# Inverse blocks of a head fetched in four transfers and spread by ScalarE and GpSimd; rotary halves exchanged by ScalarE copies

## The chip, the cores and the metric

The kernel runs on one NeuronCore of one Trainium2 chip. A core has five engines that each work through their own list of instructions in order and meet only at semaphores: TensorE (PE in the profile, with its weight loads as PEld) multiplies, VectorE (DVE), ScalarE (ACT) and GpSimd (POOL) work elementwise, and SyncE (SP) issues the transfers (DMA) between the chip's memory, HBM, and the on-chip memory, SBUF. Results of TensorE land in PSUM, a small accumulator memory. The metric is the device time of one execution in microseconds (us), taken as the median of several runs.

## The reference

One layer of a hybrid encoder on a sequence of 1024 tokens, width 1024, float32: a mixer (windowed attention beside a gated delta rule in both directions), cross-attention into 256 memory tokens, and a SwiGLU feed-forward part. What the change touches lies in the mixer. The queries and keys of the attention are rotated:

```python
def _rope(x, positions):
    ...
    x1, x2 = xf[..., :half], xf[..., half:]
    return jnp.concatenate([x1 * cos - x2 * sin, x2 * cos + x1 * sin], axis=-1)
```

and each chunk of the delta rule solves a triangular system, which the kernel does by inverting the matrix:

```python
    lower = jnp.where(strict, jnp.einsum('bhnid,bhnjd->bhnij', kb, k) * decay, 0.0)
    tmat = lower + jnp.eye(c, dtype=jnp.float32)
    ...
    sol = lax.linalg.triangular_solve(tmat, rhs, left_side=True, lower=True, unit_diagonal=True)
```

## The kernel before

Large products run as three TensorE products of a high and a low part of each operand (`split`, L99: ScalarE rounds the high part, VectorE or GpSimd subtracts the low part). The program goes through five parts: the normalized input is transposed; the delta projections (`delta_proj`) run with the preparation of each head; then comes the part that the change touches; then the scan over eight steps of 128 tokens with attention windows and the memory's keys and values in between; then the output projection, cross-attention and feed-forward part, which fill the time after some 570 us.

The part in question follows the table `ORDER_2` (L37): `L0 L1 G0 G1 A4 V A0 A1 L2 L3 W W W A2 A3 G2 G3 W`. `A` is an attention projection (`attn_proj`, 128 of the query or key columns, with the rotation), `V` the value projection, `G` a gate projection, `W` two attention windows, and `L` is `levels(h)`, which builds the inverse of the triangular matrices of head `h` (of four) out of inverses of 32 x 32 blocks. The table sets only the order in which code is written; a scheduler then orders the instructions of each engine by its own model of their times, and each engine keeps that order on the chip. All transfers of this part are issued by SP, one after the other. An instruction on any engine that waits holds up all that stand behind it on that engine.

`base_inverse(g)` (L503) inverts the 32 x 32 blocks of two heads on VectorE, in a chain of small steps (L534, L536) that ends with two scaled copies V (L538) and A (L539). Four transfers (L543) store them to `d_inv`, for g = 0 before this part and for g = 1 (heads 2 and 3) inside it. GpSimd takes part in that chain with one instruction before its steps (L528) and one after them (L537).

`levels(h)` then needs the blocks of one head in several places of 128 x 128 tiles: `D5` and `D6` (from set 0) and `Z0`, `Z1` and `m5` (from set 1). D5, D6, Z0 and Z1 exist once and are used by one head after the other; their zeros between the blocks stay from one head to the next. Each of the four row groups q of 32 partitions is fetched by a transfer of its own: 5 per q, 20 per head, 80 in all. After that come two rounds of small products (`pair`: L585, a copy `bs` by ScalarE at L587, and L591) with copies between the blocks by ScalarE and VectorE, and the finished Z0 and Z1 are stored to `d_pz` (L610), from where the scan reads them.

`attn_proj` has two halves of 512 tokens, each in a PSUM bank `pg`. The rotation multiplies with the sine (`sn`, L729), then the halves of 32 rows trade places by four transfers within SBUF (L734), while the product with the cosine (`rop`, L730) waits to be added to what comes back (L735). The sum is split into a high and a low part, and both are stored to `d_q` or `d_k` (L739), from where the windows load them as `qs`, `khi` and `klo` (L679, L625). `sn` lies in a buffer with the tag `rot`, of which two exist and which the value projection uses too, for `vT` (L745, L746).

Of the kernel before, what the change touches and what calls it, by code (L numbers as in the profile page):

```python
# [10 lines left out]
F32 = mybir.dt.float32  # L11
# [3 lines left out]
ALU = mybir.AluOpType  # L15
# [4 lines left out]
P = 128  # L20
# [3 lines left out]
NT = S // P  # L24
HALF = 512
# [7 lines left out]

ORDER_1 = "D0 P0 D1 P1 D2 B0 P2 D3 P3 B1".split()
ORDER_2 = "L0 L1 G0 G1 A4 V A0 A1 L2 L3 W W W A2 A3 G2 G3 W".split()  # L37
ORDER_3 = ("M " + "s01 W K " * 5 + "s01 K " * 3 + "s01 V V").split()
# [4 lines left out]
_ROPE_AT = len(_NAMES) * P  # L43
# [3 lines left out]
def host_constants():  # L47
    i = np.arange(P)
    blk = i // 32
    a, b = i[:, None], i[None, :]  # L50
    ba, bb = blk[:, None], blk[None, :]
    tri = {
        "ident": a == b,
        "mU": a < b,
        "mL": a > b,
        "mUi": a <= b,
        "mLi": a >= b,
        "m5": (ba // 2 == bb // 2) & (ba != bb),
        "m6": ba // 2 != bb // 2,
        "ones": a + b >= 0,  # L60
    }
    out = np.zeros((P, _NCONST), np.float32)
    for n, m in tri.items():
        out[:, _AT[n]:_AT[n] + P] = m

    out[:, _AT["band0"]:_AT["band0"] + P] = np.where(b >= a, 0.0, NEG)
    out[:, _AT["band2"]:_AT["band2"] + P] = np.where(b <= a, 0.0, NEG)
    half = np.arange(32, dtype=np.float32)
    inv = np.power(np.float32(10000.0), -half / np.float32(32)).astype(np.float32)
    out[:, _ROPE_AT] = inv[i % 32]  # L70
    out[:, _ROPE_AT + 1] = np.where(i % 64 < 32, 1.0, -1.0)
    return out


# [1 line left out]
def tile_hybrid_block(  # L76
# [4 lines left out]
    g_ffn_pre, w_gate_up, w_down, g_ffn_post, consts, out, dump=None, stop=None,  # L81
):
    nc = tc.nc
    x, mem, out = x[0], mem[0], out[0]
# [64 lines left out]
    trp = p1.enter_context(pool("trp", 2, side="right"))  # L149
# [396 lines left out]
    def levels(h):  # L546

        g, hh = h // 2, h % 2

        def fetch(dst, q, i, d):  # L550
            nc.sync.dma_start(dst, d_inv[g][i][d, hh, :, q].rearrange("c r s -> r c s"))

        m5 = tl_.tile([P, NT, 32], F32, tag="m5", name="m5", bufs=1)
        D5a, D6a, *Za = wide_sets[0]
        for q in range(4):
            r = slice(32 * q, 32 * q + 32)
            fetch(m5[r], q, 1, 1 - q % 2)
            fetch(D5a[r, :, r], q, 0, q % 2)
            fetch(D6a[r, :, r], q, 0, q // 2)
            for d in range(2):  # L560
                fetch(Za[d][r, :, r], q, 1, d)

        def part(b):
            c4 = slice(4 * b, 4 * b + 4)

            def wide(name):
                return tl_.tile([P, 4, P], F32, tag=name, name=name, bufs=2)

            L5, L6 = wide("L5"), wide("L6")
            D5, D6, Z = D5a[:, c4], D6a[:, c4], [z[:, c4] for z in Za]  # L570
            Ul = wide("Ul")
            nc.sync.dma_start(Ul, d_u[g][hh, c4].rearrange("c p n -> p c n"))
            yield
            p_ = small().rearrange("p (c n) -> p c n", c=4)
            for j in range(4):
                nc.tensor.transpose(p_[:, j, :], Ul[:, j, :], ident)
            nc.vector.tensor_tensor(L5, p_, bc(cm["m5"], 1, (P, 4, P)), ALU.mult)
            nc.vector.tensor_tensor(L6, p_, bc(cm["m6"], 1, (P, 4, P)), ALU.mult)

            def pair(lt, mv, dd, w):  # L580

                yield
                p_ = small()[:, 0:4 * w].rearrange("p (c n) -> p c n", c=4)
                for c in range(4):
                    nc.tensor.matmul(p_[:, c, :], lt[:, c, :], mv[:, c, :], start=True, stop=True)  # L585
                bs = tl_.tile([P, 4, 64], F32, tag="bs", name="bs", bufs=2)[:, :, 0:w]
                nc.scalar.copy(bs, p_)  # L587
                yield
                p_ = small()[:, 0:4 * w].rearrange("p (c n) -> p c n", c=4)
                for c in range(4):  # L590
                    nc.tensor.matmul(p_[:, c, :], dd[:, c, :], bs[:, c, :], start=True, stop=True)  # L591
                return p_

            p_ = yield from pair(L5, m5[:, c4, :], D5, 32)
            z5 = tl_.tile([P, 4, 32], F32, tag="z5", name="z5", bufs=2)
            nc.scalar.mul(z5, p_, -1.0)
            nc.vector.transpose(D6[32:64, :, 0:32], z5[0:32])
            nc.vector.transpose(D6[64:96, :, 96:128], z5[96:128])
            nc.vector.tensor_copy(Z[1][32:64, :, 0:32], z5[32:64])
            nc.vector.tensor_copy(Z[0][64:96, :, 96:128], z5[64:96])  # L600
            mov6 = tl_.tile([P, 4, 64], F32, tag="mov6", name="mov6", bufs=2)
            nc.scalar.copy(mov6[0:64], Z[1][0:64, :, 0:64])
            nc.vector.tensor_copy(mov6[64:128], Z[0][64:128, :, 64:128])
            nc.scalar.copy(Z[0][0:32, :, 32:64], z5[0:32])
            nc.scalar.copy(Z[1][96:128, :, 64:96], z5[96:128])
            p_ = yield from pair(L6, mov6, D6, 64)
            nc.scalar.mul(Z[0][0:64, :, 64:128], p_[0:64], -1.0)
            nc.vector.tensor_scalar(Z[1][64:128, :, 0:64], p_[64:128], -1.0, None, ALU.mult)
            for d in range(2):
                nc.sync.dma_start(d_pz[g][d][c4, :, hh, 1].rearrange("c p n -> p c n"), Z[d])  # L610

        together([part(b) for b in range(2)])
# [108 lines left out]
    def attn_proj(ct):  # L721
        pp = proj(w_in[:, ct * P:(ct + 1) * P])
        dst = [t[ct * P:(ct + 1) * P, :] if ct < 4 else t for t in (d_q if ct < 4 else d_k)]
        for hf in range(2):
            sl = slice(hf * HALF, (hf + 1) * HALF)
            rop = trp.tile([P, HALF], F32, tag="rop", name="rop")
            sn = trp.tile([P, HALF], F32, tag="rot", name="sn")
            rot = trp.tile([P, HALF], F32, tag="rot2", name="rot2")
            nc.vector.tensor_tensor(sn, pp[hf], sinT[:, sl], ALU.mult)  # L729
            nc.vector.tensor_tensor(rop, pp[hf], cosT[:, sl], ALU.mult)  # L730

            for q in range(4):
                o = 32 * (q ^ 1)
                nc.sync.dma_start(rot[32 * q:32 * q + 32], sn[o:o + 32])  # L734
            nc.vector.tensor_tensor(rop, rop, rot, ALU.add)  # L735
            hl = [trp.tile([P, HALF], F32R, tag=t, name=t) for t in ("qhi", "qlo")]
            split(*hl, rop)
            for t, o in zip(hl, dst):
                nc.sync.dma_start(o[:, sl], f32(t))  # L739
# [623 lines left out]
    def fetch(dst, r, ch, k, n):  # L1363
        return nc.sync.dma_start(dst[:, k:k + n], wv[:, k:k + n, r, ch * 512:(ch + 1) * 512])
# [160 lines left out]
```

## Time and profile before

| what | us |
|---|---|
| median of 3 runs (lowest, highest) | 1551.69 (1547.02, 1553.25) |
| the profiled execution, its own time | 1555.78 |
| its span from first to last instruction | 1554.1 |
| TensorE busy in the span | 1497.3 |
| VectorE busy | 1055.9 |
| ScalarE busy | 719.6 |
| GpSimd busy | 308.3 |

An engine's busy time counts its computing instructions, not waits or the issue of transfers. The page of a profile lists the busy time of each engine, a strip of 40 equal slices, the DMA queues, the chain of waits (what released what, followed back from the last instruction), the costliest groups of instructions and the issues of transfers. Other views list the waits, single instructions in order of time, or the work in chosen stretches of the span, with the clock that TensorE was granted there (1.00 is full speed). "SPq" is SP issuing a transfer. A row such as `L735 DVE TENSOR_TENSOR rop<-rop,rot ... x10: 679/688/693` gives line, engine, operation, what is written from what, how often, and the shortest, median and longest duration in ns.

### The profile page before, as it was taken

The numbers are of one execution on the slowest core, as the hardware profiler recorded it, in microseconds if no ns is written. First come the engines' busy times: TensorE is split into PE (matmuls) and PEld (weight loads), VectorE is DVE, ScalarE is ACT, GpSimd is POOL, SyncE is SP. The second block draws the span as 40 slices with busy tenths as digits, with TensorE's granted clock in tenths as the row PEclk, the third lists the DMA queues.
The fourth block names the chain that finished last, engine by engine and source line by source line (L and its number), as shares of the span: only waits on it lengthen the run. The fifth ranks groups of instructions, "written<-read, shape, count | busy, mean of one in ns | idle before, by whom it ended". The sixth has DMA issues, their size and how long they took to land.

```text
span 1554.1 us, 20931 instructions
## 1 busy us (share of the span) xinstructions
PE 1497.3 (96%) x7451; PEld 1258.1 (81%) x7451; DVE 1055.9 (68%) x1750; ACT 719.6 (46%) x1380; POOL 308.3 (20%) x305
## 2 busy tenths in 40 slices
PE   6999999898899999999999999999999999999998
PEld 5888888787899877888888777888888888888786
DVE  6777898766898766443447367776867554687665
ACT  6666552246556755454335574332323332454532
POOL 2000110000003201163102221433533333000021
PEclk9999999997999999999999999999999999999999
DMA  6244456867987584354213264344434334863354
GB/s 211 69 136 128 125 157 160 217 179 245 319 278 247 164 283 165 119 190 148 82 55 123 85 200 141 111 135 129 134 122 132 102 102 141 288 193 102 108 175 165
DMA packets 267366, 247.16 MB, mean 159 GB/s; under 512 B 39016, under 2 KB 204797, under 8 KB 267261
## 3 DMA queue, kind: packets, MB, share of 16 engines
q1 hardware_dynamic: 267261, 245.82, 50.7%
q8 instruction: 59, 0.97, 0.3%
q14 instruction: 46, 0.38, 0.1%
HBM read 173.65 MB, written 69.50 MB: 156 GB/s over the span
## 4 chain that ended last, share of the span: by engine, by line
PE 80%; DVE 6%; DMA 6%; ACT 3%; issue 2%; SPq 2%; POOL 0%; DVEq 0%; POOLq 0%; ACTq 0%
PE pg L261 13%; PE pmg L1016 10%; PE pD L1196 8%; PE pE L1196 8%; PE pA L1196 6%; PE pcq L261 6%; PE pdX L1386 6%; PE pdA L1386 4%; PE pB L1196 4%; PE psc L785 2%; PE pdX L1479 2%; PE pdD L1386 2%; DMA wraw<-in_w_ckv_dram 2%; PE pcs L1102 1%; PE pco L1128 1%
## 5 line engine op out<-in xcount | busy, mean ns | idle before, releaser
L102 ACT CAST whi<-wraw 128x1024 fp32r<-128x1024 f32 x108 | 113.5, 1051 | 173.3 <-PE pg L261 36.0
L103 DVE TENSOR_TENSOR wlo<-wraw,whi 128x1024 fp32r<-128x1024 f32 x78 | 95.5, 1225 | 77.7 <-ACT whi L102 75.0
L261 PE MATMUL pg<-hhi,whi 128*128 128x512 f32 x352 | 140.8, 401 | 0.2 <-DVE rop L730 0.2
L261 PE MATMUL pg<-hhi,wlo 128*128 128x512 f32 x352 | 140.2, 399 | 0.0
L261 PE MATMUL pg<-hlo,whi 128*128 128x512 f32 x352 | 139.9, 398 | 0.0
L1016 PE MATMUL pmg<-whi,b 128*128 128x512 f32 x384 | 118.4, 394 | 0.4 <-ACT b L102 0.4
L1196 PE MATMUL pA<-s,whi 128*128 128x512 f32 x352 | 109.5, 392 | 1.4 <-ACT m L1213 1.4
L103 POOL TENSOR_TENSOR wlo<-wraw,whi 128x1024 fp32r<-128x1024 f32 x30 | 73.8, 2460 | 143.3 <-ACT whi L102 143.2
L1016 PEld LDWEIGHTS pmg<-whi,b 128*128 128x128 f32 x384 | 71.3, 188 | 15.2 <-ACT b L102 1.3
L261 PEld LDWEIGHTS pg<-hhi,whi 128*128 128x128 f32 x352 | 67.3, 192 | 14.0 <-DVE rop L730 0.7
L261 PEld LDWEIGHTS pg<-hlo,whi 128*128 128x128 f32 x352 | 67.2, 191 | 13.2
L261 PEld LDWEIGHTS pg<-hhi,wlo 128*128 128x128 f32 x352 | 67.2, 191 | 13.1
L1196 PEld LDWEIGHTS pA<-s,whi 128*128 128x128 f32 x352 | 65.3, 188 | 15.2 <-ACT m L1213 2.0
L1386 PE MATMUL pdX<-dhl,whi 128*128 128x512 f32 x264 | 76.1, 390 | 1.5 <-DVE zv L1441 0.8
L1016 PE MATMUL pmg<-wlo,b 128*128 128x512 f32 x192 | 71.5, 392 | 0.0
L1196 PE MATMUL pA<-s,wlo 128*128 128x512 f32 x176 | 68.7, 392 | 1.1 <-DVE wlo L103 1.1
L102 ACT CAST whi<-araw 128x1024 fp32r<-128x1024 f32 (+1 forms) x36 | 35.4, 984 | 69.9 <-PE pdX L1386 27.6
L1273 POOL TENSOR_TENSOR act<-act,up 128x512 f32<-128x512 f32 x33 | 50.1, 1519 | 89.1 <-DVE up L1272 53.1
L103 DVE TENSOR_TENSOR wlo<-araw,whi 128x1024 fp32r<-128x1024 f32 (+1 forms) x36 | 40.8, 1133 | 38.4 <-ACT whi L102 38.3
L286 DVE SCALAR_TENSOR_TENSOR acc<-cp,cols,acc 128x1024 f32<-128x1024 f32 x48 | 61.5, 1282 | 1.5 <-ACT acc L284 0.8
L1386 PEld LDWEIGHTS pdX<-dhl,whi 128*128 128x128 f32 x264 | 49.3, 188 | 12.8 <-issue 1.1
L1246 DVE TENSOR_TENSOR sr<-sr,wraw 128x512 f32<-128x512 f32 x22 | 37.8, 1716 | 29.8 <-POOL sr L1245 29.8
(409 smaller groups left out, 3976.7 us busy)
## 6 DMA issues: line engine op xcount, KB each, us to landing
wraw<-in_w_gate_up_dram SPq DMA_DIRECT2D x52, 512.0 KB, 4.0
kv<-d_kv SPq DMA_DIRECT2D x32, 512.0 KB, 6.6
wraw<-in_w_in_dram SPq DMA_DIRECT2D x22, 512.0 KB, 5.5
b<-in_w_down_dram SPq DMA_DIRECT2D x20, 512.0 KB, 6.8
araw<-d_as SPq DMA_DIRECT2D x20, 512.0 KB, 3.8
pz<-d_pz SPq DMA_DIRECT2D x32, 256.0 KB, 6.8
wraw<-in_w_ckv_dram SPq DMA_DIRECT2D x16, 512.0 KB, 6.4
wraw<-in_w_out_dram SPq DMA_DIRECT2D x16, 512.0 KB, 4.3
```

The source lines that it names most:

```text
L102: nc.scalar.copy(hi, src)
L103: (eng or nc.vector).tensor_tensor(lo, src, f32(hi), ALU.subtract)
L261: nc.tensor.matmul(p_, w[:, k, :], ah[a][:, k, :], start=(k == 0 and i == 0), stop=(k == nk - 1 and i == 2))
L286: nc.vector.scalar_tensor_tensor(acc, cp[:, t:t + S], taps[t], acc, ALU.mult, ALU.add)
L785: nc.tensor.matmul(out[:, d, h, :], lt[:, d, h, :], rt[:, d, h, :], start=True, stop=True)
L1016: nc.tensor.matmul(pp[t], act[a][:, k, tt], w_[:, kk, :], start=(k == 0 and i == 0), stop=(k == KT - 1 and i == 2))
L1102: nc.tensor.matmul(pp[:, t2_, :], q[a][:, ct, tt], kr_[b_][:, ct, :], start=(j == 0 and i == 0), stop=(j == 1 and i == 2))
L1196: nc.tensor.matmul(out_, w[a][:, k, :], xx[b_][:, k, :], start=(start and k == 0 and i == 0), stop=(k == HK - 1 and i == 2), skip_group_ch ...
L1246: nc.vector.tensor_tensor(s[1], s[0], a_[:, 0:HK], ALU.subtract)
L1273: nc.gpsimd.tensor_tensor(o_, o_, up, ALU.mult)
L1386: nc.tensor.matmul(banks[t], a[:, k - k0, tt], w, start=(first and k == 0 and i == 0), stop=(k == NB - 1 and i == 2), skip_group_check=not ...
L1479: nc.tensor.matmul(X[t], a[:, k], w[:, k0 + k], start=False, stop=(k0 + k == NB - 1 and i == 2), skip_group_check=True)
```

## The change

The blocks of a head now come in four transfers instead of 20: each of the four sets (two of set 0, two of set 1) is fetched whole, 128 partitions x 8 chunks x 32, into a tile `c` of which four exist (`LC = 4`). From there 8 GpSimd copies put them into D5 and D6, and 12 ScalarE copies into m5, Z0 and Z1, each copy 32 partitions x 256 elements. For four heads that is 16 transfers in place of 80, 32 GpSimd copies and 48 ScalarE copies.

The rotation now begins with four ScalarE copies of 32 partitions x 512 out of PSUM, which write each group of 32 rows to the partitions of its partner group. VectorE then multiplies the copy with the sine in place, and adds as before. For five projections of two halves that is 40 ScalarE copies in place of 40 transfers; VectorE keeps three multiplications or additions per half. The sign column of the constants is turned around, since the sine is now taken at the place where the row arrives. The tile of tag `rot2` is gone.

```diff
+LC = 4
...
-    out[:, _ROPE_AT + 1] = np.where(i % 64 < 32, 1.0, -1.0)
+    out[:, _ROPE_AT + 1] = np.where(i % 64 < 32, -1.0, 1.0)
...
-        def fetch(dst, q, i, d):
-            nc.sync.dma_start(dst, d_inv[g][i][d, hh, :, q].rearrange("c r s -> r c s"))
+        def fetch(i, d):
+            t = tl_.tile([P, NT, 32], F32, tag="c", name="c", bufs=LC)
+            nc.sync.dma_start(t, d_inv[g][i][d, hh].rearrange("c b r s -> (b r) c s"))
+            return t
 
         m5 = tl_.tile([P, NT, 32], F32, tag="m5", name="m5", bufs=1)
         D5a, D6a, *Za = wide_sets[0]
+        cw = [fetch(0, d) for d in range(2)]
         for q in range(4):
             r = slice(32 * q, 32 * q + 32)
-            fetch(m5[r], q, 1, 1 - q % 2)
-            fetch(D5a[r, :, r], q, 0, q % 2)
-            fetch(D6a[r, :, r], q, 0, q // 2)
-            for d in range(2):
-                fetch(Za[d][r, :, r], q, 1, d)
+            nc.gpsimd.tensor_copy(D5a[r, :, r], cw[q % 2][r])
+            nc.gpsimd.tensor_copy(D6a[r, :, r], cw[q // 2][r])
+        cz = [fetch(1, d) for d in range(2)]
+        for q in range(4):
+            r = slice(32 * q, 32 * q + 32)
+            nc.scalar.copy(m5[r], cz[1 - q % 2][r])
+        for d in range(2):
+            for q in range(4):
+                r = slice(32 * q, 32 * q + 32)
+                nc.scalar.copy(Za[d][r, :, r], cz[d][r])
...
-            sn = trp.tile([P, HALF], F32, tag="rot", name="sn")
-            rot = trp.tile([P, HALF], F32, tag="rot2", name="rot2")
-            nc.vector.tensor_tensor(sn, pp[hf], sinT[:, sl], ALU.mult)
-            nc.vector.tensor_tensor(rop, pp[hf], cosT[:, sl], ALU.mult)
-
+            rot = trp.tile([P, HALF], F32, tag="rot", name="rot")
             for q in range(4):
                 o = 32 * (q ^ 1)
-                nc.sync.dma_start(rot[32 * q:32 * q + 32], sn[o:o + 32])
+                nc.scalar.copy(rot[32 * q:32 * q + 32], pp[hf][o:o + 32])
+            nc.vector.tensor_tensor(rop, pp[hf], cosT[:, sl], ALU.mult)
+            nc.vector.tensor_tensor(rot, rot, sinT[:, sl], ALU.mult)
             nc.vector.tensor_tensor(rop, rop, rot, ALU.add)
```

Since the scheduler orders everything anew, the change also moves instructions that it doesn't name. In the rows below the lines of the changed kernel count 1 more than before up to the change and 7 to 9 more behind it; a name's number tells buffers apart.

First, ScalarE where the blocks of head 0 and the rotation of the first projection stand. Before:

```order
L102 CAST whi<-wraw 128x1024
L758 ACT_TABLE_LOAD
L758 ACTIVATE gt<-pg 128x512
L102 CAST whi<-wraw 128x1024 x2
L587 COPY bs<-ps 128x4x32
L746 COPY vT<-pg 128x512
L587 COPY bs<-ps 128x4x32
```

And now:

```order
L739 COPY rot<-pg 32x512 x4
L103 CAST qhi<-rop 128x512
L103 CAST whi<-wraw 128x1024
L739 COPY rot<-pg 32x512 x4
L566 COPY m_2128<-c 32x256 x2
L570 COPY Z_2122<-c 32x8x32 x4
L753 COPY vT<-pg 128x512
L566 COPY m_2128<-c 32x256 x2
L570 COPY Z_2123<-c 32x8x32 x4
```

The copies of the rotation (`rot`) and of the blocks (`m`, `Z`) stand ahead of `vT`, where ScalarE had two roundings of weights.

Second, SP between the store of the inverse blocks for heads 2 and 3 and the loads of the first window. Before:

```order
L543 DMA d_inv_113<-A 64x1024
L543 DMA d_inv_114<-A 64x1024
L739 DMA d_q_98<-qhi 128x512
L551 DMA m_2832<-d_inv_114 32x8x32
L551 DMA D_2120<-d_inv_113 32x8x32
L551 DMA m_2832<-d_inv_114 32x8x32
L551 DMA D_2120<-d_inv_113 32x8x32
L739 DMA d_q_99<-qlo 128x512
L551 DMA D_2120<-d_inv_113 32x8x32
L551 DMA m_2832<-d_inv_114 32x8x32 x2
L551 DMA D_2120<-d_inv_113 32x8x32
L679 DMA khi<-d_k_100 64x1024 x2
```

And now:

```order
L544 DMA d_inv_113<-A 64x1024
L544 DMA d_inv_114<-A 64x1024
L553 DMA c<-d_inv_113 128x8x32 x2
L553 DMA c<-d_inv_114 128x8x32 x2
L688 DMA khi<-d_k_100 64x1024 x2
L688 DMA klo<-d_k_101 64x1024 x2
L634 DMA qs<-d_q_98 64x4x128
```

Eight fetches of blocks and two stores of queries between the inverse blocks and the window's keys have become four fetches; the window's loads still stand behind the store of the inverse blocks.

Third, ScalarE late in the part, where the blocks of head 3 are due, behind head 2's last copies. Before (the blocks themselves came by transfers):

```order
L667 COPY ao<-pow 64x512
L758 ACTIVATE gt<-pg 128x512
L642 ACT_TABLE_LOAD
L642 ACTIVATE sc,ssum<-sc,nm 128x384 x4
L646 ACTIVATE es<-es 128x4
L587 COPY bs<-ps 128x4x32 x2
L102 CAST ph<-ptw 128x512 x2
L758 ACT_TABLE_LOAD
L758 ACTIVATE gt<-pg 128x512
```

And now:

```order
L616 ACTIVATE Z_2122<-ps 64x4x64 x2
L676 COPY ao<-pow 64x512
L765 ACT_TABLE_LOAD
L765 ACTIVATE gt<-pg 128x512
L570 COPY Z_2122<-c 32x8x32 x4
L570 COPY Z_2123<-c 32x8x32 x4
L103 CAST ph<-ptw 128x512
L655 ACT_TABLE_LOAD
L655 ACTIVATE es<-es 128x4
L651 ACTIVATE sc,ssum<-sc,nm 128x384 x4
L765 ACT_TABLE_LOAD
L765 ACTIVATE gt<-pg 128x512
```

Eight copies into Z0 and Z1 now stand on ScalarE among the windows' exponentials, and the function tables are loaded more often: 10 times over the part where there were 6.

## The prediction

> **What bounds the kernel now.** I read the page first: busy times and the chain of waits.
>
> ```profile
> PE 1497.3 (96%) x7451; PEld 1258.1 (81%) x7451; DVE 1055.9 (68%) x1750; ACT 719.6 (46%) x1380; POOL 308.3 (20%) x305
> PE 80%; DVE 6%; DMA 6%; ACT 3%; issue 2%; SPq 2%; POOL 0%; DVEq 0%; POOLq 0%; ACTq 0%
> ```
>
> TensorE is the bound over the whole kernel, so an edit elsewhere pays only where TensorE stands still or runs at a lowered clock. The change lies between 228 and 384 us. The view by stretches shows what is to be had there; the columns are TensorE, weight loads, VectorE, ScalarE, GpSimd (busy us), then the granted clock, the DMA share and GB/s.
>
> ```profile
> 228.00:250.00 22.00, 22.00 (x103) 18.16 (x101) 18.25 (x33) 2.11 (x2) 2.26 (x1) 1.00 0.68 155
> 250.00:270.00 20.00, 17.97 (x94) 15.57 (x94) 17.08 (x40) 6.98 (x17) 0.00 (x0) 0.83 0.70 193
> 270.00:290.00 20.00, 20.00 (x112) 17.18 (x112) 15.97 (x39) 3.73 (x9) 0.16 (x1) 1.00 0.71 194
> 290.00:310.00 20.00, 16.82 (x93) 13.97 (x91) 13.56 (x25) 7.84 (x18) 0.00 (x0) 1.00 0.88 228
> 310.00:330.00 20.00, 18.25 (x92) 15.94 (x92) 10.13 (x27) 4.67 (x15) 0.20 (x1) 0.83 0.69 160
> 330.00:350.00 20.00, 19.77 (x112) 16.94 (x112) 16.28 (x42) 11.62 (x29) 0.59 (x1) 1.00 0.68 203
> 350.00:370.00 20.00, 19.27 (x117) 17.39 (x116) 11.47 (x35) 12.41 (x30) 0.20 (x1) 0.89 0.66 183
> 370.00:384.00 14.00, 10.80 (x43) 8.44 (x43) 8.29 (x21) 8.66 (x20) 2.15 (x5) 0.54 0.85 278
> 228.00:384.00 156.00, 144.88 (x755) 123.59 (x754) 111.04 (x256) 58.03 (x137) 5.56 (x10) 0.90 0.73 196
> ```
>
> TensorE is idle for 156 - 144.88 = 11.1 us, and the clock takes more: 0.17 x 20 in each of two stretches, 0.11 x 20 and 0.46 x 14, together 15.4 us. So at most 26.5 us can be won here. The lowered clock follows the idle places (250:270, 290:330, the end): a stop costs itself and then a few us at half speed.
>
> The issuing engine, SP, is what these stops have in common. Its rows for the fetches and the rotation (shortest/median/longest ns per issue):
>
> ```profile
> L551 SPq DMA_DIRECT2D D<-d_inv x32: 390/452/874, 239.4 to 352.3; - x32
> L551 SPq DMA_DIRECT2D Z<-d_inv x32: 302/449/1042, 240.4 to 359.9; - x32
> L551 SPq DMA_DIRECT2D m<-d_inv x16: 320/467/1333, 238.6 to 325.6; - x16
> L734 SPq DMA_DIRECT2D rot<-sn x40: 507/588/1240, 251.1 to 340.6; - x40
> ```
>
> By the medians that is 14.5 + 14.4 + 7.5 + 23.5 = 59.8 us of issuing in some 125 us. The waits from 228 to 385 us name what is late for it (us in total, times, longest), and the chain of waits names two longer places:
>
> ```profile
> DVE rop L735 <- DMA rot<-sn: 7.4, 5, 2.8
> ACT vT L746 <- DMA rot<-sn: 4.3, 1, 4.3
> PE psw L633 <- DMA qs<-d_q: 3.9, 1, 3.9
> 306.21 5.30 DMA qs<-d_q
> 311.75 1.19 PE psw L633 x4
> ...
> 355.25 4.63 DMA d_gate<-gt
> 359.89 2.87 DMA Z<-d_inv
> ```
>
> **The change part by part.** The sum is made against the profiled execution, 1555.78 us with a span of 1554.1; it lies 4.1 us above the median of the runs, and a difference is carried over to the median unchanged.
>
> *SP.* 120 issues go. 16 fetches of 128 KB come; the nearest row is the block load at L515 (64 KB in pieces of the same 128 bytes):
>
> ```profile
> L515 SPq DMA_DIRECT2D V<-d_u x8: 604/628/1056, 138.1 to 235.2; - x8
> ```
>
> At 0.45 to 1.06 us each they take 7 to 17 us, 10 by the median. SP is relieved of some 50 us. That is no gain in itself: it ends the waits above, and the next things that are late must be found place by place.
>
> *vT at 253 us.* vT waited for the rotation's transfers, since it shares the buffer tag. The 2.0 us stop of TensorE and 0.17 x 20 = 3.4 us of clock go, 5.4 us at that place. But TensorE runs into the first window's product (psw) later on, which waits for `qs`; what is won at 253 us only lengthens that wait, so I book nothing here.
>
> *The first window.* By the order of SP, its loads still stand behind the store of VectorE's inverse for heads 2 and 3. So the question is when that chain ends. VectorE stops in it for the rotation's transfers:
>
> ```profile
> 255.18 0.69 DVE L735 TENSOR_TENSOR rop<-rop,rot 128x512 f32<-128x512 f32 x1 [1.45 <-DMA rot<-sn]
> 272.98 0.69 DVE L735 TENSOR_TENSOR rop<-rop,rot 128x512 f32<-128x512 f32 x1 [0.75 <-DMA rot<-sn]
> 289.04 0.69 DVE L735 TENSOR_TENSOR rop<-rop,rot 128x512 f32<-128x512 f32 x1 [2.77 <-DMA rot<-sn]
> ```
>
> Together 5.0 us go: VectorE's own work per half stays at three operations of 0.69. Against that stand 16 GpSimd copies for heads 0 and 1 that fall into the chain, and GpSimd and VectorE hold each other up, as a later place shows:
>
> ```profile
> 1005.51 1.30 POOL L1247 TENSOR_TENSOR sr<-wraw 128x512 f32<-128x512 f32 x1
> 1005.59 1.77 DVE L1246 TENSOR_TENSOR sr<-sr,wraw 128x512 f32<-128x512 f32 x1 [3.93 <-POOL sr L1245]
> 1007.99 0.69 DVE L1248 TENSOR_TENSOR sr<-wraw,sr 128x512 f32<-128x512 f32 x1
> ```
>
> The same operation takes 0.69 alone and 1.77 beside GpSimd. A GpSimd copy of 256 elements does not occur; bounds are a fill of 1024, scaled to a quarter (0.24), and an addition of 256 with two inputs (0.74):
>
> ```profile
> L719 POOL MEMSET Z<- 128x1024 f32 x2 | 1.8, 950 | 0.0
> L853 POOL TENSOR_TENSOR ol<-ol,of x12: 732/739/746, 471.7 to 508.9; 128x256 f32<-128x256 f32 x12
> ```
>
> I take 0.45 (one input, but strided): 16 x 0.45 = 7.2 us of GpSimd, of which VectorE may lose anything from 0 to 7.2. I take 1.5, as most copies should fall beside operations that read PSUM or in VectorE's waits. Net 5.0 - 1.5 = 3.5 us earlier. The eight fetches that stood ahead of the keys give way to four that wait for the whole store to land, which I set equal. The order also puts 5 products of a projection more ahead of the window (254 instead of 249), 1.1 us by a run of 94 of them:
>
> ```profile
> 228.38 21.36 PE pg L261 x94
> ```
>
> Window: -3.5 - 1.1 = -4.6; at best 5.0 + 1.1 and the issue of the eight fetches, 3.6, that is -9.7; at worst, with all 7.2 lost, +1.1.
>
> *Head 3.* Its Z blocks before:
>
> ```profile
> 355.83 5.10 SPq L551 DMA_DIRECT2D Z<-d_inv  x8
> ```
>
> The last of the eight landed at 362.76, 6.9 us after the first was issued, with a gate store's landing of 4.63 between them; products, copies and the last d_pz store of this part follow from there. Now the blocks lie in SBUF early, and eight ScalarE copies remain. The nearest rows are 32 x 128 and 64 x 256 within SBUF, and out of PSUM 64 x 512 for the rotation:
>
> ```profile
> L604 ACT COPY Z<-z 32x128 f32<-32x128 f32 x8 | 2.4, 296 | 0.2
> L602 ACT COPY mov<-Z x8: 406/407/408, 258.9 to 363.9; 64x256 f32<-64x256 f32 x8
> L667 ACT COPY ao<-pow x16: 582/584/587, 347.4 to 572.4; 64x512 f32<-64x512 f32 x16
> ```
>
> 8 x 0.40 = 3.2: head 3 gains 3.7 us (0 to 6.9).
>
> *ScalarE.* 48 x 0.40 + 40 x 0.584 = 42.6 us are added, and four table loads of 1.28:
>
> ```profile
> L642 ACT ACT_TABLE_LOAD x2 | 2.6, 1283 | 0.0
> d_pz<-Z SPq DMA_DIRECT2D x16, 256.0 KB, 4.6
> ```
>
> ScalarE goes from 58.0 to about 106 of 156 us. Up to 290 us it worked 12.8 of 62 us: there the copies cost nothing, covered by TensorE's projections. If that cover were gone, a half's four copies would hold its bank 2.3 us longer, against the 5.4 us that 24 products of 0.227 us take to fill the next. Later on the engine is busier; I book one table load on the path, +1.3.
>
> *Rotation behind the first window.* VectorE's two other waits of 7.4 - 5.0 = 2.4 us go, but TensorE stood for only 0.23 us of 330:350. Half of it, -1.2, between 0 and -2.4.
>
> Sum: -4.6 - 3.7 + 1.3 - 1.2 = -8.2. The profiled span would be 1546, the median 1551.7 - 8.2 = **1543.5**. Taking all ends at once (-9.7 - 6.9 - 2.4, and +1.1 with all four table loads, 5.1) gives -19 to +6; the later parts keep their work.
>
> **The rivals.**
>
> *GpSimd holds VectorE up.* If VectorE loses 6 of the 7.2 us, the chain ends where it ended and the window stands at 311 us. For it: the pair of rows at 1005 us, where the loss of 1.08 is most of GpSimd's 1.30. Against it: the operations beside the copies are short, and the copies come in two bursts. The sum is then -8.2 + 4.5 = -3.7, 1548, no measurable difference. The Trainium skill, "SBUF — State Buffer", section "SBUF: two separate sides", has this as a rule: the port pair that VectorE and GpSimd share is an exclusive lock, which a VectorE operation with two SBUF inputs and a GpSimd operation that reads SBUF hold for the whole instruction. The pair of rows agrees; whether a one-input copy does the same, no row of this trace shows.
>
> *All of SP's delays go* and the windows' loads come early enough that TensorE no longer stops before 330 us. Then the 6.8 us of clock in 250:270 and 310:330 go too, with the 2.0 + 3.2 + 1.8 us of idle time, 13.8, and head 3's 3.7 and the rotation's 1.2 with them: -18.7, 1533. Against it: the inverse chain still stands ahead of the window's loads.
>
> *ScalarE becomes the bound of the late part* (slower). From 310 to 384 us it worked 37.4 of 74 us. Added are up to 16 rotation copies (9.3), 24 block copies (9.6) and four table loads (5.1): 61 of 74. It takes instructions strictly in order, and its Z copies for heads 2 and 3 wait until the former head's d_pz stores have landed, 4.6 us each by the row above. Behind them stand the copies `bs` and the rounded `ph` for TensorE. If nothing can be done meanwhile, 2 x 4.6 + 5.1 = 14.3 us are lost on the path and TensorE runs at half clock for longer; against -8.2 - 1.3 that is +4.8, and with another 3.4 us of lowered clock +8.2: 1560. It decides from the point where ScalarE's work plus its waits exceed the time that TensorE's remaining projections cover, as in 370:384, where ScalarE worked 8.66 of 14 us and TensorE stood. Against it: VectorE and TensorE set the pace in 310:330, where ScalarE did 4.67.
>
> **How the numbers follow.** A measurement here can tell about 0.5%, 7.8 us, from no change. The forecast (0.44) lies just on that bound: by the spread of its terms two thirds of it count as faster, 0.30, and 0.14 as no difference. All delays gone: 0.17, faster. GpSimd holds VectorE up: 0.11, no difference. ScalarE as the bound: 0.28, slower. So faster 0.47, same 0.25, slower 0.28. The range reaches to the outer cases, 1531 to 1562; the forecast's own is 1534 to 1552.
>
> **What would show it.** In the changed profile vT no longer waits for a transfer, VectorE's addition for the rotation has no DMA as releaser, and 250:270 has a clock of 1.00. The first psw starts about 307 us instead of 311.75; if it is at 311 or later, with small steps of VectorE's chain drawn out beside GpSimd's copies, the first rival holds. Block copies on ScalarE should last 0.3 to 0.4 us. If ScalarE's waits for d_pz landings stand at the head of its list and TensorE idles more than 3.2 us at the end of the part, the slower rival holds. The forecast is wrong if the later parts, from the scan on, change by more than 3 us.

## The result and the profile after

| kernel | median us (lowest to highest, runs) |
|---|---|
| before | 1550.51 (1546.00 to 1555.14, 22) |
| the change | 1555.64 (1549.86 to 1562.01, 22) |

The change is slower: 1.0035 times the time before, 95% interval 1.0024 to 1.0045, some 5 us. That lies within the 0.5% called no difference above; the forecast of 1543.5 us had the wrong sign.

The two first profiles can't be set against each other in total. The one of before is among its longest executions (1555.78), the one after among its shortest (1551.68). Places are compared instead, and both were profiled once more.

First the page of the changed kernel, its busy times:

```profile
PE 1494.7 (96%) x7451; PEld 1254.6 (81%) x7451; DVE 1059.3 (68%) x1750; ACT 764.5 (49%) x1472; POOL 321.7 (21%) x337
```

ScalarE has 44.9 us more than before and GpSimd 13.4, about what the copies were priced at. Some stretches of the changed part (TensorE, weight loads, VectorE, ScalarE, GpSimd, then granted clock, DMA share, GB/s):

```profile
228.00:250.00 22.00, 21.49 (x104) 17.66 (x102) 18.20 (x29) 12.51 (x25) 6.60 (x9) 0.98 0.97 230
250.00:270.00 20.00, 20.00 (x110) 17.33 (x109) 18.99 (x47) 12.40 (x28) 3.20 (x6) 0.93 0.38 99
...
290.00:310.00 20.00, 17.15 (x89) 14.33 (x88) 15.16 (x31) 13.64 (x30) 3.43 (x8) 0.93 0.92 215
310.00:330.00 20.00, 19.00 (x90) 15.70 (x89) 8.49 (x20) 13.99 (x29) 0.20 (x1) 0.90 0.88 245
...
350.00:370.00 20.00, 18.49 (x113) 17.17 (x111) 11.97 (x36) 15.02 (x35) 0.40 (x2) 0.83 0.16 50
...
228.00:384.00 156.00, 145.95 (x764) 123.00 (x762) 114.62 (x263) 107.10 (x236) 20.95 (x43) 0.92 0.63 167
```

TensorE no longer idles in 250:270, and its idle time over the part is 10.1 us instead of 11.1. The clock of 250:270 rises from 0.83 to 0.93, not to the 1.00 that was named as a sign; TensorE had stood for 0.5 us in the stretch before. So the change does at its beginning most of what it was meant to do. The new rows are the copies (shortest/median/longest ns, first and last start):

```profile
L739 ACT COPY rot<-pg x40: 574/577/582, 229.2 to 320.8; 32x512 f32<-32x512 f32 x40
L570 ACT COPY Z<-c x32: 400/403/408, 244.3 to 351.5; 32x256 f32<-32x256 f32 x32
L566 ACT COPY m<-c x16: 400/404/406, 243.5 to 331.8; 32x256 f32<-32x256 f32 x16
...
L561 POOL COPY D<-c x16: 392/398/860, 243.7 to 333.6; 32x256 f32<-32x256 f32 x16
L562 POOL COPY D<-c x16: 390/394/1296, 244.5 to 345.6; 32x256 f32<-32x256 f32 x16
```

The view of the waits from 228 to 385 us (total, times, longest) has no wait of vT or of `rop` for a transfer any more. New are ScalarE's waits for the landing of `c` and of `d_pz`:

```profile
ACT m L566 <- DMA c<-d_inv: 9.2, 5, 5.5
...
ACT Z L570 <- DMA d_pz<-Z: 3.1, 3, 1.5
...
PE psw L642 <- DMA qs<-d_q: 2.3, 1, 2.3
```

VectorE's chain and the first window stand in the order of time as follows (start, us):

```profile
288.03 2.07 DVE L539 TENSOR_TENSOR V<-A,bB 128x1024 f32<-128x1024 f32 x1
...
290.56 1.20 DVE L540 TENSOR_TENSOR A<-A,bB 128x1024 f32<-128x1024 f32 x1
```

```profile
307.94 0.55 PE L642 MATMUL psw<-khi,qs 128*128 128x256 f32 x1 [2.33 <-DMA qs<-d_q]
```

V began at 290.17 before, A ended at 295.12 and the window began at 311.75. All three are now 2 to 4 us earlier. Where these microseconds go is seen by milestones, all from the traces (two profiled executions of each kernel; "rotation alone" is explained below):

| us | before | change | rotation alone |
|---|---|---|---|
| first window product | 311.8, 311.0 | 307.9, 308.1 | 310.2, 308.2 |
| head 1's last store to `d_pz` | 310.9, 310.1 | 312.2, 312.3 | 317.0, 315.0 |
| last projection product | 358.6, 357.4 | 353.6, 354.7 | 353.5, 351.6 |
| head 2's last store | 350.2, 348.8 | 346.3, 347.0 | 347.2, 345.3 |
| head 3's last store | 373.4, 369.3 | 376.0, 377.1 | 367.4, 365.5 |
| scan's first product | 382.8, 378.3 | 382.9, 383.9 | 374.9, 373.0 |

The change is 3 to 5 us ahead at the first window's and the last projection's product, and at the scan's beginning some 5 us behind the second profile of before. The stretch between the last stores of heads 2 and 3 takes 29.7 and 30.1 us; it took 23.2 and 20.5 before. From the scan's first product to the end of the span the profiles take 1171.2 and 1167.7 us before, 1167.1 and 1169.1 with the change. The two kernels differ there by no more than two executions of one, so the loss lies ahead of the scan.

### The profile page after: what moved, and what is told of

Read it like the earlier page. It is cut to its first block, busy times and chain, and to the rows that moved or that the text cites. A ratio compares the mean times of both kernels' runs of the same rounds, so it can differ in the third digit from the quotient of the medians.

```text
span 1550.0 us, 20928 instructions
## 1 busy us (share of the span) xinstructions
PE 1494.7 (96%) x7451; PEld 1254.6 (81%) x7451; DVE 1059.3 (68%) x1750; ACT 764.5 (49%) x1472; POOL 321.7 (21%) x337
## 4 chain that ended last, share of the span: by engine, by line
PE 63%; DMA 6%; DVE 5%; ACT 5%; issue 2%; POOL 1%; SPq 1%; DVEq 0%; POOLq 0%; ACTq 0%
PE pmg L1023 10%; PE pD L1203 8%; PE pE L1203 8%; PE pA L1203 6%; PE pcq L262 6%; PE pdX L1393 6%; PE pdA L1393 4%; PE pB L1203 4%; PE psc L792 3%; PE pdD L1393 2%; DMA wraw<-in_w_ckv_dram 2%; PE pcs L1109 1%; PE pco L1135 1%; PE pdX L1486 1%; DVE wlo L104 1%
## 5 line engine op out<-in xcount | busy, mean ns | idle before, releaser
L262 PEld LDWEIGHTS pg<-hhi,wlo 128*128 128x128 f32 x352 | 67.0, 190 | 13.3
```

The source lines that it names most:

```text
L262: nc.tensor.matmul(p_, w[:, k, :], ah[a][:, k, :], start=(k == 0 and i == 0), stop=(k == nk - 1 and i == 2))
```

## The experiments

**The two kernels once more**, one profile each: the change, and the kernel before.

> The changed kernel once more, for a second profile: its first profile was one of its fastest executions (1551.7 against a median of 1555.6). Theory A: from the last projection to the scan's first product again some 29 us, and where this execution is slower than the first it is slower in that part (scan's first product later than 383 us). Rival: the part before the scan is as in the first profile within 1 us and the difference between executions comes from later parts.

> The kernel before once more, for a second profile: its first was one of its slowest executions (1555.8 against a median of 1550.5). Theory A: the scan's first product comes earlier than in the first profile (378 to 381 us instead of 382.8). Rival: it comes at 382 to 384 us again, and the faster execution is faster later on.

The change took 1554.67 us and repeats its first profile's places within 1.2 us (second numbers of the table). The kernel before took 1547.68; its part ends 4.5 us earlier than in the first profile. There TensorE's clock was lowered for 17.1 us from 365.7 on, here for 6.8. So of the two profiles of before, the prediction was built on the one with the slower end of the part.

**Each part of the change alone.** Rotation alone: the change with the 80 direct fetches put back. Blocks alone: the rotation of before with the new blocks, where memory allows only three tiles `c` and one `rot2`.

```diff
-            rot = trp.tile([P, HALF], F32, tag="rot", name="rot")
+            sn = trp.tile([P, HALF], F32, tag="rot", name="sn")
+            rot = trp.tile([P, HALF], F32, tag="rot2", name="rot2", bufs=1)
```

> The changed kernel with the 80 fetches of blocks put back, so that only the rotation is new (ScalarE copies in place of 40 transfers). Theory A (the loss sits in ScalarE's block copies: its Z copies wait in line for the landing of the former head's store, with the windows' exponentials behind them, and the extra function-table loads): this kernel has none of those copies and is not slower than before, ratio 0.994 to 1.001; the first window's product starts earlier than 311.8 us and the time from the last projection to the scan's first product stays at 24 us. Theory B (the loss sits in the rotation's ScalarE copies, which hold up the small copies bs and z of the levels): slower than before, 1.002 to 1.006, and that time grows towards 29 us.

> The kernel before with only the blocks changed (four transfers per head, spread by GpSimd and ScalarE); the rotation goes by transfers as before. To fit in memory three tiles c instead of four, and one buffer of tag rot2 instead of two. Theory A: slower than before, 1.002 to 1.007, with the Z copies' waits for d_pz and 27 to 31 us from the last projection to the scan's first product. Theory B: not slower, 0.995 to 1.001.

> The rotation alone once more, as the version that beats both: 0.994 to 0.9965, if its first result holds on this chip.

Rotation alone: 1541.97 us, ratio 0.9950 (0.9936 to 0.9965); on another occasion 1543.07, 0.9946 (0.9929 to 0.9964). It beats both kernels, and the theory that the rotation's ScalarE copies are the loss falls. Blocks alone: 1560.78, 1.0073 (1.0060 to 1.0087), but its single `rot2` makes VectorE wait 16.6 us for the rotation, so its size says little. What counts is the difference of the change and the rotation alone: the blocks' part costs 1.0035 - 0.9950 = 0.85%, some 13 us (0.89% with the second measurement of the rotation).

**Other engines for the copies.** In the change, the twelve copies per head that ScalarE makes go elsewhere: all to GpSimd; only m5 to GpSimd; only Z to GpSimd; only Z to VectorE.

```diff
-            nc.scalar.copy(m5[r], cz[1 - q % 2][r])
+            nc.gpsimd.tensor_copy(m5[r], cz[1 - q % 2][r])
...
-                nc.scalar.copy(Za[d][r, :, r], cz[d][r])
+                nc.gpsimd.tensor_copy(Za[d][r, :, r], cz[d][r])
```

> The changed kernel with all 20 block copies of a head on GpSimd; ScalarE has none. Theory A1 (the loss is ScalarE's strict order: block copies that wait for a landing hold up the copies bs and z, the exponentials and the rotation behind them): the wait moves to an engine on which nothing else is urgent, and the kernel comes down to the level of the rotation alone, ratio 0.993 to 0.999. Theory A2 (the loss is in the fetch: four bulk transfers that wait for the whole store, and copies behind them, whoever makes them): no better than the changed kernel, 1.002 to 1.006. GpSimd needs 80 copies of 0.39 us, 31 us in all, and VectorE would lose to them if the lock mattered: its chain's end (V) would come 2 us later or more.

> The changed kernel with only the four copies into m5 of each head on GpSimd; the eight Z copies stay on ScalarE. In the changed kernel's profile the m5 copies of head 2 wait 5.5 us for the landing of their fetch with head 1's bs behind them. If that wait is what counts: 0.995 to 1.000. If the Z copies count (behind the landing of d_pz): still 1.002 to 1.005.

> The changed kernel with only the eight Z copies of each head on GpSimd; the m5 copies stay on ScalarE. If the Z copies behind the landing of d_pz are what counts: 0.995 to 1.000. If the m5 copies' wait counts: 1.001 to 1.004.

> The changed kernel with the eight Z copies of each head on VectorE. Theory A1 (any engine with urgent work in line behind the waiting copy loses): VectorE is busier than ScalarE until 300 us, so no better than the changed kernel, 1.001 to 1.006. If it is ScalarE's load and not the order that counts (VectorE copies within SBUF take less: 0.22 us for 32 x 128): 0.996 to 1.001.

| copies moved | us | ratio (interval) | scan begins |
|---|---|---|---|
| none (the change) | 1555.64 | 1.0035 (1.0024 to 1.0045) | 382.9 |
| all to GpSimd | 1564.48 | 1.0095 (1.0070 to 1.0120) | 394.7 |
| m5 to GpSimd | 1557.83 | 1.0057 (1.0035 to 1.0079) | 387.5 |
| Z to GpSimd | 1549.83 | 1.0004 (0.9990 to 1.0018) | 378.7 |
| Z to VectorE | 1557.20 | 1.0048 (1.0032 to 1.0063) | 385.0 |

An idle engine does not make copies free. With all on GpSimd the waits of that kernel read:

```profile
POOL m L566 <- DMA c<-d_inv: 19.8, 4, 7.1
...
POOL Z L570 <- DMA d_pz<-Z: 15.8, 5, 8.1
```

This kernel is slower than either theory allowed. The copies are released by different events (the landing of `c`, that of `d_pz`, TensorE's last product of the former head) and stand in one line: four D copies (314.48 us) start without a wait of their own, right behind m copies that had waited 7.1 and 3.4 us for their fetches. Moving Z to GpSimd helps, by 0.3%; moving it to VectorE does not.

**Which heads, which blocks.** Four kernels with the change's rotation, and the new way of fetching only for heads 0 and 1; only for heads 2 and 3; for D5 and D6 of every head; for m5, Z0 and Z1 of every head. All other blocks come by direct fetches.

```diff
+        if h < 2:
...
+        else:
+            for q in range(4):
+                r = slice(32 * q, 32 * q + 32)
+                direct(m5[r], q, 1, 1 - q % 2)
+                direct(D5a[r, :, r], q, 0, q % 2)
...
```

> The change, but the 40 fetches of heads 2 and 3 go straight into place again; heads 0 and 1 keep the four transfers and the copies. Late theory (the loss comes from heads 2 and 3, whose copies wait for landings in strict-order lines of ScalarE and GpSimd while TensorE has little left to do): as good as the rotation alone, ratio 0.995 to 0.997, last projection to scan about 21 us. Load theory (each head's fetches and copies cost the same wherever they stand): half the loss, about 0.999. Order theory (the new order of everything is what costs, not the copies): not between the two, 1.002 or more, or a new place of loss.

> The converse: heads 0 and 1 with the 40 direct fetches, heads 2 and 3 with four transfers and copies each. Late theory: as the change, ratio 1.002 to 1.005, last projection to scan 28 to 30 us. Load theory: about 0.999.

> Of every head only D5 and D6 come by two whole fetches and GpSimd copies; m5, Z0 and Z1 by 12 direct fetches; rotation by ScalarE as in the change. If the loss is in ScalarE's line (Z and m5 copies that wait for d_pz and c among other work): ratio 0.995 to 0.997. If it is in GpSimd's line or in the extra step of the fetch for D: 1.000 to 1.004.

> The converse: m5, Z0 and Z1 by two whole fetches and 12 ScalarE copies, D5 and D6 by 8 direct fetches. If the loss is in ScalarE's line: ratio 1.001 to 1.004. If it is in GpSimd's line: 0.995 to 0.998. About 0.999 in both this and the former: both halves cost alike.

| new way for | us | ratio (interval) | scan begins | over rotation alone |
|---|---|---|---|---|
| heads 0, 1 | 1548.43 | 0.9989 (0.9978 to 1.0000) | 378.5 | +0.39% |
| heads 2, 3 | 1546.99 | 0.9983 (0.9972 to 0.9994) | 377.0 | +0.33% |
| D5, D6 | 1550.82 | 1.0005 (0.9995 to 1.0015) | 380.1 | +0.55% |
| m5, Z0, Z1 | 1556.01 | 1.0040 (1.0026 to 1.0053) | 386.3 | +0.90% |

By heads the loss halves, and the halves add up to 0.72 of 0.85%: the late theory, by which heads 0 and 1 cost nothing, falls. By blocks it does not add up: either kind alone costs more than half, together 1.45%. ScalarE's copies alone cost as much as the whole change, although the 40 issues of m5, Z0 and Z1 on SP are saved there, too.

**Head 3, and the copies for TensorE.** In the traces most of the loss shows between head 2's and head 3's last stores, so parts of it were taken away there: head 3 fetched directly; its Z copies on GpSimd; its four copies `bs` on VectorE; first and third together; and `bs` of heads 2 and 3 on VectorE.

```diff
-                nc.scalar.copy(bs, p_)
+                (nc.vector.tensor_copy if h == 3 else nc.scalar.copy)(bs, p_)
```

> The change, but head 3's blocks go straight into place by 20 fetches; heads 0 to 2 as in the change. ScalarE keeps the change's order there, with the exponentials of two windows and two gates ahead of head 3's copy bs, and only the eight Z copies and the wait before them (3.3 + 0.7 us) are gone. Head-3 theory (the change's whole loss lies between head 2's last store to d_pz and head 3's, 29.7 us in the change against 20.2 with the rotation alone): if it is the copies and their wait, that stretch shrinks by about 4 us to 26 and the ratio is 1.000 to 1.002; if the order of exponentials and table loads ahead of bs costs as much again, it stays there and no more than 4 us come back. Load theory (every head's copies cost the same): a quarter of the loss comes back, 2 us, ratio about 1.002.

> The change, but head 3's eight Z copies on GpSimd; the other heads as in the change. By the order, head 3's bs then stands ahead of the exponentials of the last windows and behind two gates, two exponentials' groups and their table loads. Head-3 theory: the stretch from head 2's last store to head 3's shrinks from 29.7 to 20 to 23 us, and the ratio falls to 0.996 to 0.999. Load theory: the copies only change engine, ratio 1.002 to 1.004.

> The change, but head 3's four copies bs (two of each round) on VectorE; ScalarE's order is the change's with these copies taken out. In the change TensorE has finished the first product for bs at 354.8 us, bs starts at 358.25 behind four exponentials, two table loads and a gate. Order theory (bs held in ScalarE's line costs the rest of head 3's delay): bs at 355 to 356, TensorE's stop of 1.5 us before L600 gone, the stretch from head 2's last store to head 3's 25 to 28 us instead of 29.7, ratio 1.001 to 1.003. Copies theory (only the eight Z copies and their wait count): unchanged, 29 to 30 us and 1.0025 to 1.0045.

> Both for head 3: blocks fetched directly, and its four copies bs on VectorE; heads 0 to 2 as in the change. If the two parts add up: stretch 21 to 24 us, ratio 0.998 to 1.000. If they are one and the same delay: as with the direct fetches alone, 26 to 27 us and 1.0005 to 1.002.

> The change, but the eight copies bs of heads 2 and 3 on VectorE. In the change these eight stand, finished by TensorE and not yet begun, 24.8 us in all in ScalarE's line, against 2.8 us with the rotation alone. If that standing itself is the loss: below 8 us in all, the scan begins 4 to 8 us earlier than in the change (382.9 us), ratio 0.998 to 1.001. If z, Z and the exponentials behind the same table loads hold up the heads anyway: the scan begins at 381 us or later, ratio 1.0015 to 1.0045.

| kernel | us | ratio (interval) | head 2's to head 3's last store | scan begins |
|---|---|---|---|---|
| the change | 1555.64 | 1.0035 (1.0024 to 1.0045) | 29.7 | 382.9 |
| head 3 direct | 1551.47 | 1.0012 (1.0001 to 1.0023) | 26.7 | 379.9 |
| head 3's Z on GpSimd | 1552.23 | 1.0015 (1.0003 to 1.0027) | 29.0 | 384.6 |
| head 3's `bs` on VectorE | 1553.01 | 1.0022 (1.0010 to 1.0033) | 28.4 | 383.2 |
| both | 1552.60 | 1.0020 (1.0010 to 1.0031) | 27.2 | 380.5 |
| `bs` of heads 2, 3 on VectorE | 1555.18 | 1.0044 (1.0031 to 1.0058) | 23.8 | 381.3 |
| rotation alone | 1541.97 | 0.9950 (0.9936 to 0.9965) | 20.2 | 374.9 |

With head 3 fetched directly the stretch is 3.0 us shorter and the time 0.23% lower. The rest does not come back. The copies on GpSimd and `bs` on VectorE give back 0.1 to 0.2% (their intervals overlap with the change's), and the two measures don't add up. In the last kernel `bs` no longer stands in ScalarE's line and the stretch is 5.9 us shorter, but the last projection product begins at 360.2 us (353.6 in the change) and the time is that of the change. Two of the eight `bs` now stand on VectorE behind a product that waits 6.0 us for ScalarE's exponentials (343.40 us), and TensorE waits longer for another copy of ScalarE, the rounded `ph`, from 290 to 385 us:

```profile
PE pow L673 <- ACT ph L103: 5.1, 2, 4.0
```

It was 2.5 us in the change. So the waits shift to other pieces of ScalarE's line, and the standing of `bs` in it is not by itself the loss: if it were, this kernel was to come to 0.998 to 1.001. The eight `bs` still stand 13.3 us in all, where less than 8 was expected, so the test is not a clean one.

## Why the prediction was wrong

**Right, by its steps.** vT's wait is gone: its transposes begin at 246.6 us instead of 255.8. VectorE's addition no longer waits for a transfer; four times its product with the cosine (L740) stands until ScalarE's copies are done, 4.4 us in all, of which 0.7 fall into the chain to the window. The window was to start about 307 and starts at 307.9. The copies last 0.58 and 0.40 us, as priced. Without the blocks the sum was -5.0 - 1.1 - 1.2 = -7.3 us; the rotation alone measured -0.50 and -0.54% of 1550, -7.8 and -8.4. The gain came elsewhere than stated, though: its window starts only 1 to 4 us earlier than before, and the rest is won later, up to the scan; that the sums agree is in part luck.

**GpSimd and VectorE** hold each other up for a short time only. GpSimd's and VectorE's rows of the changed kernel:

```profile
245.79 1.31 POOL L561 COPY D<-c 32x256 f32<-32x256 f32 x2
247.16 0.39 POOL L562 COPY D<-c 32x256 f32<-32x256 f32 x1
```

```profile
245.41 0.38 DVE L535 TENSOR_TENSOR tmpb<-A 128x30 f32<-128x30 f32 x1
...
246.31 0.40 DVE L537 TENSOR_TENSOR A<-A,tmpb 128x30 f32<-128x30 f32 x1
246.75 0.42 DVE L535 TENSOR_TENSOR tmpb<-A 128x58 f32<-128x58 f32 x1
```

The step of 128x30 takes 0.38 here and 0.18 at 287.54, where GpSimd is idle. Up to 248.5 us six steps take 1.0 us more than the same steps before, and beside the two later bursts of copies (from 255.53 and 268.69 us) VectorE loses some 0.3 and 0.5 us more: 1.8 in all, against the 1.5 booked. The Trainium skill, "SBUF — State Buffer", section "SBUF: two separate sides", has the port pair that the two engines share held by a VectorE operation with two SBUF inputs against a GpSimd operation that reads SBUF, and these rows agree for a copy with one input, which the prediction had left open. The rival's loss of 6 us is not there.

**Wrong: the steps "Head 3" and "ScalarE".** Head 3 was to gain 3.7 us, with ScalarE at +1.3 for one table load on the path. There was no such gain to be had: the fetches of Z whose last landing (362.76 us) the prediction priced were not what head 3 waited for. From 228 to 390 us before, the waits name one for a fetch of blocks, and the second profile of before names none:

```profile
DVE mov L603 <- DMA Z<-d_inv: 0.4, 1, 0.4
```

The chain of waits shows the transfer at its whole length (2.87 us); waited for were its last 0.4.

Instead of a gain, the stretch of head 3 is 6.5 to 9.6 us longer than before and 9.5 us longer than with the rotation alone, and the blocks' part as a whole, booked at -3.7 + 1.3 + 1.5 = -0.9 us, costs 13. I counted the copies' durations and hid them behind TensorE's work; I did not ask what stands behind them in ScalarE's line at each place. Head 2 shows how work comes to stand there. ScalarE's rows in the change:

```profile
317.31 1.66 ACT L570 COPY Z<-c 32x256 f32<-32x256 f32 x4 [1.50 <-DMA d_pz<-Z]
318.98 2.35 ACT L739 COPY rot<-pg 32x512 f32<-32x512 f32 x4
321.36 1.65 ACT L570 COPY Z<-c 32x256 f32<-32x256 f32 x4
323.02 1.28 ACT L655 ACT_TABLE_LOAD   x1
...
324.54 1.28 ACT L765 ACT_TABLE_LOAD   x1
325.84 0.60 ACT L765 ACTIVATE gt<-pg 128x512 f32<-128x512 f32 x1
326.45 1.28 ACT L651 ACT_TABLE_LOAD   x1
327.75 0.51 ACT L651 ACTIVATE sc<-sc,nm 128x256 f32<-128x256 f32 x1
...
329.73 0.24 ACT L596 COPY bs<-ps 128x128 f32<-128x128 f32 x1
```

and with the rotation alone:

```profile
316.94 2.35 ACT L731 COPY rot<-pg 32x512 f32<-32x512 f32 x4
319.31 1.28 ACT L647 ACT_TABLE_LOAD   x1
320.61 0.21 ACT L647 ACTIVATE es<-es 128x4 f32<-128x4 f32 x1
322.35 0.51 ACT L643 ACTIVATE sc<-sc,nm 128x256 f32<-128x256 f32 x1 [1.54 <-DVE nm L641]
...
324.45 0.27 ACT L588 COPY bs<-ps 128x128 f32<-128x128 f32 x1
```

The first window's exponentials (`sc`) begin 5.4 us later: 0.4 from the later start, 3.3 for eight Z copies, 2.6 for two more table loads, 0.6 for a gate that now stands ahead, less 1.5 that ScalarE waited for VectorE anyway. And `bs`, behind them, is 5.3 us later. TensorE had finished the products for it:

```profile
321.63 0.97 PE L594 MATMUL ps<-m,L 128*128 128x32 f32 x8
...
323.34 0.97 PE L594 MATMUL ps<-m,L 128*128 128x32 f32 x8
```

By 322.6 us the first was done, and its copy began at 329.73: 7.1 us in the line, where the rotation alone has 1.2. Summed over the eight `bs` of heads 2 and 3 the standing is 24.8 us in both profiles of the change, 2.8 in both of the rotation alone, 5.7 and 5.1 before.

The sum of this standing is a sign of the new order and not a price. Head 2's four `bs` stand 18.9 us, and its stretch (from head 1's last store to its own) is 4 us longer than with the rotation alone; head 3's stand 5.9, and its stretch is 9.5 us longer. Over the kernels tried the sum does not follow the time either: it is 3.7 us with all copies on GpSimd, the slowest, and 17.1 with the new way for heads 2 and 3 only, one of the faster ones.

A good part of what TensorE loses is clock. From 228 us to the scan's first product it stands still for 10.1 and 12.2 us with the change, 7.5 and 9.4 with the rotation alone, some 2.6 us more. The mean granted clock over the same stretch is 0.92 and 0.93 against 0.95 and 0.97; as time (what the clock lacks to 1.00, times the length) that is 12.4 and 10.9 us against 7.3 and 4.4, some 5 to 6 us more. The last stretch of the change, of the rotation alone and of the kernel with head 3 fetched directly (columns as above; it reaches into the scan):

```profile
353.00:385.00 32.00, 27.09 (x148) 22.93 (x146) 19.32 (x55) 22.55 (x59) 2.35 (x6) 0.79 0.36 104
```

```profile
353.00:385.00 32.00, 27.20 (x179) 23.96 (x178) 26.01 (x70) 23.67 (x60) 2.22 (x6) 0.89 0.73 246
```

```profile
353.00:385.00 32.00, 25.32 (x162) 21.32 (x161) 22.06 (x64) 24.04 (x64) 2.35 (x6) 0.95 0.55 158
```

In the change the 16 products that had waited 1.51 us for head 3's `bs` (358.65 us) take 3.60 us; with head 3 fetched directly they wait 0.60 and take 1.97. More than half of the 3.0 us that this kernel gains in the stretch is this difference in speed.

As far as the traces show, three things come together, of which the prediction had one each in different places: the extra step (a block is fetched, lands, and is copied), the wait for the former head's stores inside a strict line, and the order that the scheduler then chooses around longer ScalarE work, with 9 table loads from 228 to 395 us against 5 before and 7 with the rotation alone. In head 3, where the copies alone were taken away in the same order, ScalarE's row behind them reads

```profile
351.17 0.59 ACT L103 CAST ph<-ptw 128x512 fp32r<-128x512 f32 x1 [2.97 <-PE ptw L681]
...
357.70 0.43 ACT L609 COPY bs<-ps 128x128 f32<-128x128 f32 x2
```

so the time of the copies (3.3 us) turned into waiting, and `bs` came 0.6 us sooner (358.25 in the change). The copies' own time was hidden there, as predicted; the order was not.

**The slower rival** (ScalarE bounds the late part) named the right engine and place, and priced it at +4.8 to +8.2 us; +5.1 was measured. So the size is luck: its terms were not those that decide, and of its two signs one is met, barely. TensorE idles for 3.4 us from 370 to 384, where more than 3.2 was named; but the landings of `d_pz` don't head ScalarE's waits. It had two of them at 4.6 us each; ScalarE waited 3.1 us for them and 9.2 for `c`. Four table loads on the path would be 5.1 us, but the kernel with Z on GpSimd has only 5 loads and is 0.5% slower than the rotation alone, which has 7. What it lacked is that exponentials of the first windows would stand behind the copies, too, and that heads 0 and 1 count as well.

**Open.** That the blocks' part costs 13 us, and that ScalarE's copies of m5 and Z alone can cost as much, is measured; by which step they do it is argued from the traces and not shown. How the 13 us divide between the work added and the order that follows from it was not settled. Every kernel tried was ordered anew, and no run held the order of all engines fixed while the copies were taken away. It also stays open how much a mere change of order moves the time: no kernel was tried that has the same work in another order. A second set of Z tiles, which would take the wait for `d_pz` away, was not tried. The kernel with m5, Z0 and Z1 alone is also not explained by `bs`: 8.8 us of standing, and yet 1.0040; its clock is lowered for 20.5 us from 357.7 on.

## What to carry to other kernels

A copy moved to an engine with free time is not free: it stands in a strict line, and what stands behind it waits with it. In this kernel neither the busy time nor any one kind of wait told the price; the dates of a few milestones, in two profiles of each kernel, told where it was paid. A wait that an edit is to remove has to be looked up first: here the fetch that was to give 3.7 us held up 0.4. Before trading transfers for copies, list for each copy what releases it and what follows it on its engine, and keep copies with different releasers out of one line with work that another engine waits for. And split such a change: here one half alone is 0.5% faster, and the other half loses more than that.

## What the runs showed of the hardware

- A GpSimd copy of 32x256 (0.39 us) takes no longer than ScalarE's (0.40); beside VectorE's work it took up to 0.86 (L561, 245.79) and 1.30 (L562, 269.12, beside a subtraction of 128x1024).
- ScalarE's copies of 32x512 out of PSUM (0.577 us) take the same as its copies of 64x512 (0.582 before); both write to other partitions than they read. The number of rows is not seen in the time.
- A change of ScalarE's function table costs the load and nothing more: the load at 326.45 starts 0.01 us after the gate ends, and the exponential starts 1.30 us later. The Trainium skill, "ScalarE: Activation LUTs", section "What ACT_TABLE_LOAD costs", adds a drain to each change and comes to about 2.66 us; these rows don't show it, and the measurement decides here.
- The two profiled executions of the kernel before differ by 8.1 us, at a mean granted clock of 0.983 and 0.990.
